# A decoder layer in split fp32: both MLP products by 2x2 blocks with seven block products, the squared activations kept in DRAM, the gate as a stage of its own

## The chip, the cores and the metric

The kernel runs on one core of one Trainium2 chip. The metric is device microseconds of one execution; the time before is the median of three runs. Engine names are those of the profile: PE is TensorE's matmuls, PEld its weight loads, DVE VectorE, ACT ScalarE, POOL GpSimd, SP the queue of SyncE that issues all DMAs.

## The reference

One layer of a hybrid decoder on 2048 tokens of 1024 channels. A token mixer (RWKV-7 beside a pooling mixer, both gated) gives `x1`; then come the squared-ReLU MLP, a gated embedding and a final norm. The change touches what follows the mixer:

```python
h = rmsnorm(x, g_mlp)                                   # 2048 x 1024
x = x + jnp.square(jax.nn.relu(h @ w_ff1)) @ w_ff2      # w_ff1 1024 x 4096, w_ff2 4096 x 1024
h = rmsnorm(x, g_ple)
x = x + jax.nn.sigmoid(h @ w_ple_gate) * (p @ w_ple_proj)   # p 2048 x 256
return rmsnorm(x, g_final)
```

## The kernel before

Every matmul operand is a pair of fp32r tiles, the rounded value ("hi", made by an ACT cast) and the rest ("lo", a subtraction on DVE or POOL). `mm3` multiplies a stationary pair by a moving pair in three matmuls: hi by hi, hi by lo, lo by hi. A moving operand is 512 columns wide, so all large matmuls are 128x128 by 128x512.

The order of PE is the order of the code (`manual_schedule`); a scheduler orders the other engines, each of which then works strictly in its order. PSUM has eight banks: four of tag `d` (`dps`), two of `rp` (`rps`), two of `rc` (`cps`).

The mixer fills the first half of the time. Its last part, `stage_B` of the fourth block of 512 tokens, projects with `yx` and `big` as operands (24 matmuls a group) and writes `x1` to DRAM (`x1D`). Between its groups, `head0` loads, normalises, transposes and splits the first eight tiles of 128 tokens into `hT2`.

Then the tokens go in two halves (`blk`) of 1024, eight tiles each. In a half, `w_ff1` is taken in 32 column tiles. `ff1` computes one tile for 1024 tokens (2 x 24 matmuls), squares on ACT and DVE and splits the result into `rt`. After four such tiles, `w_ff2`'s four row tiles are multiplied with them (192 matmuls) and added on DVE into `xa`, which holds the half's `x1` in SBUF. Weights come raw from DRAM and are split by `wsplit`: hi on ACT, lo half on DVE and half on POOL (L1099), into rings of two (`w1`) and four (`w2`) buffers.

In the last chunk of a half, `xa`'s tiles are normalised with `g_ple`, transposed between the matmuls and put back into `hT2`. The gate follows in the same half: `gate_mm` 24 matmuls and `put` 6 for each tile and each 512 columns, then tanh, product, sum, final norm and store. The weights of the gate are split in each half, in the rings of `w1`, `w2` and `rt`. The next half's norms and transposes lie between the gate's second eight groups.

Of the kernel before, what the change touches and what calls it, by code (L numbers as in the profile page):

```python
# [18 lines left out]
P = 128  # L19
T = 2048  # L20
# [78 lines left out]
def hybrid_kernel(ctx, tc, consts, x, p, g_mix, w_in, mu_shift, w0, w_decay_up, a0, w_aaa_up,  # L99
# [94 lines left out]


    with ExitStack() as c1:
        const = c1.enter_context(tc.tile_pool(name="const1", bufs=1, side="left"))
        fg = c1.enter_context(tc.tile_pool(name="fg", bufs=1, side="left"))

# [61 lines left out]
        c1r = ExitStack()  # L261
# [104 lines left out]
        big = fg.tile([P, 2, 8, TB], FR, name="big")  # L366
        yx = fg.tile([P, 2, 4, TB], FR, name="yx")
# [36 lines left out]
        def stage_A(b, nxt):  # L404
# [39 lines left out]
            def shifted(zi, m):  # L444
# [7 lines left out]
                ze = fg.tile([P, 15 + TB], F32, name="ze", tag="pl", bufs=3)  # L452
# [50 lines left out]
            for g, w in reversed(list(enumerate(WINS))):  # L503
# [3 lines left out]
                zp = fg.tile([P, W], F32, name="zp", tag="pl", bufs=3)  # L507
# [4 lines left out]
                while sh < w:  # L512
                    lo += sh
                    nx = fg.tile([P, W], F32, name="zs", tag="pl", bufs=3)
                    DVE.tensor_tensor(nx[:, lo:W], cur[:, lo:W], cur[:, lo - sh:W - sh], ALU.add)
                    cur, sh = nx, sh * 2
# [556 lines left out]
        gb = gvec(g_mlp[0])  # L1073

        def head0():
            xts = {}
            for j in range(NJ + 1):
                if j < NJ:
                    xts[j] = fg.tile([P, D], F32, name="xt", tag="wr", bufs=WR)
                    SP.dma_start(out=xts[j], in_=x1D[j * P:(j + 1) * P, :])  # L1080
                    norm_tile(fg, xts[j], gb, xts[j], dict(tag="t2k", bufs=5))
                    yield
                if j > 0:
                    transpose_split(xts.pop(j - 1), hT2, (j - 1) * P, cps)
                    yield

        w1p = ctx.enter_context(tc.tile_pool(name="w1p", bufs=1, side="right", reuse_waits="tile"))
        w1v = w_ff1[0].rearrange("(k p) c -> p k c", p=P)

        def wsplit(pool, src, k, n, wpool, tag, bufs):  # L1090
            raw = pool.tile([P, 1024], F32, name="wr", tag="wr", bufs=WR if pool is fg else 3)
            SP.dma_start(out=raw[:, 0:k * n].rearrange("p (k n) -> p k n", n=n), in_=src)
            wf = wpool.tile([P, 2, 1024], FR, name="wf", tag=tag, bufs=bufs)
            hi = wf[:, 0, 0:k * n]
            ACT.copy(out=hi, in_=raw[:, 0:k * n])  # L1095
            ws = WS3 if pool is not fg else k * n
            for eng, c in ((DVE, slice(0, ws)), (POOL, slice(ws, k * n))):
                if c.start < c.stop:
                    eng.tensor_tensor(wf[:, 1, c], raw[:, c], hi.bitcast(F32)[:, c], ALU.subtract)  # L1099
            return wf.rearrange("p s (k n) -> p s k n", n=n)  # L1100

        def w1tile(pool, m):
            return wsplit(pool, w1v[:, :, m * P:(m + 1) * P], 8, P, w1p, "w1", 2)

        hg = head0()
        for n, y in enumerate(stage_B(NB - 1, None)):
            if n >= 24 and n % 4 == 0:
                next(hg, None)
        for _ in hg:
            pass  # L1110
        w1pre = {m: w1tile(fg, m) for m in range(2)}
    f2 = ctx.enter_context(tc.tile_pool(name="f2", bufs=1, side="left", reuse_waits="tile"))
    if True:
        def wtile2(src, k, n, tag, bufs):
            return wsplit(f2, src, k, n, w1p if tag == "w1" else f2, tag, bufs)

        def tmp2():
            return f2.tile([P, 512], F32, name="t2", tag="t2", bufs=3)

        tjunk = dict(tag="t2", bufs=3)  # L1120
        w2v = w_ff2[0].rearrange("(k p) c -> p k c", p=P)
        wgv = w_ple_gate[0].rearrange("(k p) c -> p k c", p=P)
        wpv = w_ple_proj[0].rearrange("(k p) c -> p k c", p=P)
        xa = [None] * NJ

        def load_xa(blk, j):
            xa[j] = f2.tile([P, D], F32, name="xa", tag=f"xa{j}", bufs=1)
            SP.dma_start(out=xa[j], in_=x1D[blk * TC + j * P:blk * TC + (j + 1) * P, :])

        def norm_x(gbc, j, rows=None):  # L1130
            xn = f2.tile([P, D], F32, name="xn", tag="wr", bufs=3)
            src = xa[j]
            if rows is not None:
                src = xn
                SP.dma_start(out=xn, in_=x1D[rows, :])
# [11 lines left out]
        def ff1(ms, late=()):  # L1147
# [3 lines left out]
            for hf in range(TC // 512):  # L1151
# [207 lines left out]
```

## Time and profile before

| | |
|---|---|
| median of 3 runs | 3362.46 us (3361.72 to 3364.98) |
| profiled execution | 3362.13 us, span 3360.3 us, mean granted clock 0.98 |
| busy: PE, DVE, ACT, POOL | 3196.8 (95%), 2021.1 (60%), 1182.4 (35%), 950.1 us (28%) |
| moved by DMA | 485.60 MB, mean 145 GB/s |
| first half's MLP, gate | 1685 to 2361 us, 2361 to 2533 us of the span |
| second half's MLP, gate | 2533 to 3219 us, 3219 us to the end |

A row of a group reads: line, engine, operation, output<-inputs, shapes, count | busy us, mean ns of one | idle time of the engine just before them, and what ended it. Matmuls are pipelined, so the mean of one is longer than the distance of two. A row of the timeline begins with start and duration in us. In the slices a digit is the busy share in tenths.

### The profile page before, as it was taken

The numbers are of one execution on the slowest core, as the hardware profiler recorded it, in microseconds if no ns is written. First come the engines' busy times: TensorE is split into PE (matmuls) and PEld (weight loads), VectorE is DVE, ScalarE is ACT, GpSimd is POOL, SyncE is SP. The second block draws the span as 40 slices with busy tenths as digits, with TensorE's granted clock in tenths as the row PEclk, the third lists the DMA queues.
The fourth block names the chain that finished last, engine by engine and source line by source line (L and its number), as shares of the span: only waits on it lengthen the run. The fifth ranks groups of instructions, "written<-read, shape, count | busy, mean of one in ns | idle before, by whom it ended". The sixth has DMA issues, their size and how long they took to land.

```text
span 3360.3 us, 43232 instructions
## 1 busy us (share of the span) xinstructions
PE 3196.8 (95%) x15177; PEld 2620.5 (78%) x15177; DVE 2021.1 (60%) x5020; ACT 1182.4 (35%) x2406; POOL 950.1 (28%) x1162
## 2 busy tenths in 40 slices
PE   7989999999999997889899999999999999999998
PEld 6777777777878786668688888888788888888887
DVE  4489888788887879873643333333775333333375
ACT  4445544554455444431322222211332222221132
POOL 4655444344434435421111111111102111111110
PEclk9999999999999998999999999999999999999999
DMA  8866767666766567778741111110233111111021
GB/s 249 243 216 205 245 205 236 222 212 186 227 218 219 175 209 235 234 242 290 275 140 51 51 51 51 44 51 26 83 131 113 51 51 51 51 47 47 26 65 60
DMA packets 391030, 485.60 MB, mean 145 GB/s; under 512 B 168158, under 2 KB 298268, under 8 KB 367644
## 3 DMA queue, kind: packets, MB, share of 16 engines
q1 hardware_dynamic: 390812, 482.83, 45.1%
q8 instruction: 120, 1.97, 0.2%
q14 instruction: 98, 0.80, 0.1%
HBM read 363.21 MB, written 119.54 MB: 144 GB/s over the span
## 4 chain that ended last, share of the span: by engine, by line
PE 70%; DVE 14%; DMA 7%; ACT 3%; issue 3%; POOL 2%; SPq 1%; DVEq 0%; POOLq 0%; ACTq 0%
PE d L133 63%; DVE Xtmp L869 3%; PE rc L133 3%; PE rp L133 3%; DMA At<-aD 2%; DVE Xt L872 1%; ACT sq L961 1%; DMA aD<-Ast 1%; DMA wf<-wc 1%; DMA t2k<-yaD 1%; PE rp L137 1%; DVE wf L238 1%; DVE Apr L859 1%; PE rc L137 1%; SPq L789 0%
## 5 line engine op out<-in xcount | busy, mean ns | idle before, releaser
L133 PE MATMUL d<-big,wf 128*128 128x512 f32 (+1 forms) x3288 | 840.6, 403 | 17.6 <-DVE wf L238 9.2
L133 PEld LDWEIGHTS d<-big,wf 128*128 128x128 f32 x3288 | 608.9, 192 | 150.2 <-DVE wf L238 11.7
L133 PE MATMUL d<-wf,rt 128*128 128x512 f32 x3072 | 722.4, 395 | 0.0
L133 PE MATMUL d<-hT,wf 128*128 128x512 f32 x3072 | 700.1, 389 | 0.6 <-DVE hT L185 0.4
L133 PEld LDWEIGHTS d<-wf,rt 128*128 128x128 f32 x3072 | 574.9, 187 | 139.7
L133 PEld LDWEIGHTS d<-hT,wf 128*128 128x128 f32 x3072 | 576.5, 188 | 121.6 <-DVE hT L185 0.7
L1099 POOL TENSOR_TENSOR wf<-wr,wf 128x512 fp32r<-128x512 f32 x146 | 256.8, 1764 | 1396.1 <-ACT wf L1095 1394.5
L1215 DVE TENSOR_TENSOR xa<-xa,d 128x512 f32<-128x512 f32 x256 | 175.7, 686 | 410.0 <-PE d L133 409.6
L1095 ACT CAST wf<-wr 128x1024 fp32r<-128x1024 f32 x148 | 153.4, 1045 | 688.7 <-PE d L133 570.0
L1159 DVE TENSOR_TENSOR t<-t,d 128x512 f32<-128x512 f32 x128 | 87.9, 687 | 274.9 <-ACT t L1158 274.9
L869 DVE TENSOR_TENSOR Xtmp<-Xt,At 128x16 f32<-128x16 f32 (+15 forms) x512 | 238.3, 465 | 9.3
L133 PE MATMUL d<-yx,wf 128*128 128x512 f32 x768 | 210.0, 420 | 25.7 <-ACT yx L387 15.8
L133 PE MATMUL d<-wf,big 128*128 128x512 f32 x768 | 190.5, 401 | 11.0 <-DVE t2k L608 9.2
L1158 ACT ACTIVATE t<-d 128x512 f32<-128x512 f32 x128 | 76.6, 599 | 347.3 <-PE d L133 347.3
L133 PEld LDWEIGHTS d<-yx,wf 128*128 128x128 f32 x768 | 150.1, 202 | 62.1 <-ACT yx L387 17.5
L1099 DVE TENSOR_TENSOR wf<-wr,wf 128x512 fp32r<-128x512 f32 (+1 forms) x148 | 115.8, 783 | 131.3 <-ACT wf L1095 130.9
L133 PE MATMUL d<-wf,hT 128*128 128x512 f32 x768 | 183.6, 394 | 0.0
L1161 DVE TENSOR_TENSOR rt<-t,rt 128x512 fp32r<-128x512 f32 x128 | 154.0, 1203 | 45.3 <-ACT rt L1160 45.3
L133 PEld LDWEIGHTS d<-wf,big 128*128 128x128 f32 x768 | 143.0, 191 | 43.7 <-DVE t2k L608 11.1
L133 PEld LDWEIGHTS d<-wf,hT 128*128 128x128 f32 x768 | 143.9, 188 | 33.6
L872 DVE TENSOR_REDUCE Xt<-Xtmp 128x8 f32<-128x16 f32 (+15 forms) x512 | 147.5, 288 | 9.4
L238 POOL TENSOR_TENSOR wf<-wr,wf 128x640 fp32r<-128x640 f32 (+2 forms) x69 | 121.1, 1756 | 76.4 <-ACT wf L235 71.8
(225 smaller groups left out, 3921.3 us busy)
## 6 DMA issues: line engine op xcount, KB each, us to landing
wf<-wc SPq DMA_DIRECT2D x131, 1024.0 KB, 5.7
wr<-in_w_ff_dram SPq DMA_DIRECT2D x128, 512.0 KB, 4.0
wc<-wf SPq DMA_DIRECT2D x50, 1024.0 KB, 6.3
wr<-in_w_in_dram SPq DMA_DIRECT2D x51, 512.0 KB, 4.4
zD<-t2k SPq DMA_DIRECT2D x96, 256.0 KB, 4.7
zs<-zD SPq DMA_DIRECT2D x32, 640.0 KB, 6.4
At<-aD SPq DMA_DIRECT2D x32, 512.0 KB, 4.8
xt<-in_x_dram SPq DMA_DIRECT2D x28, 512.0 KB, 6.9
```

Source lines behind the costliest of these rows:

```text
L133: PE.matmul(out_, lhsT, rhs, start=start, stop=stop, **kw)
L137: PE.transpose(out_, in_, idn)
L238: eng.tensor_tensor(wf[:, 1, c], raw[:, c], hi.bitcast(F32)[:, c], ALU.subtract)
L859: DVE.tensor_tensor(pr, Ab[:, :, :, e:e + 1].broadcast_to([P, SUB, nb, lvl]), dgv[:, :, o:o + lvl].unsqueeze(1).broadcast_to([P, SUB, nb, ...
L869: DVE.tensor_tensor(tmp[:, :, :, 0:n], Xt[:, :, 0:n].unsqueeze(2).broadcast_to([P, MCOL, FS, n]), At[:, 0:n, r:n].rearrange("p s r -> p r ...
L872: DVE.tensor_reduce(Xt[:, :, r:n].unsqueeze(3), tmp[:, :, :, 0:n], AX.X, ALU.add)
L1095: ACT.copy(out=hi, in_=raw[:, 0:k * n])
L1099: eng.tensor_tensor(wf[:, 1, c], raw[:, c], hi.bitcast(F32)[:, c], ALU.subtract)
L1158: ACT.activation(out=t, in_=ps, func=AF.Relu)
L1159: DVE.tensor_tensor(t, t, ps, ALU.mult)
L1161: DVE.tensor_tensor(rt[:, 1, cs], t, rt[:, 0, cs].bitcast(F32), ALU.subtract)
L1215: DVE.tensor_tensor(xa[j][:, ns], xa[j][:, ns], ps, ALU.add)
```

## The change

Write the three matrices of a product as 2x2 blocks, with the tokens of a half split into two times 512 (indices `e`), and K and N split in two. Seven block products of sums replace the eight. For the left matrix A and the right B, with S1 = A21 + A22, S2 = S1 - A11, S3 = A11 - A21, S4 = A12 - S2:

P1 = A11 B11, P2 = A12 B21, P3 = S4 B22, P4 = A22 (B21 - t2), P5 = S1 (B12 - B11), P6 = S2 t2, P7 = S3 (B22 - B12), where t2 = B22 - B12 + B11. The result's blocks are P1 + P2; U2 + P5 + P3; U3 + P4; U3 + P5, with U2 = P1 + P6 and U3 = U2 + P7.

First product, 32 pairs (2 halves x 16): B's blocks alternate in column tiles of 128, so that a pair's two tiles stand side by side in memory (256 columns). The seven left operands of 512 columns stay split in SBUF ("home": four new tiles, `yx`, and both halves of `big`); each of a pair's seven products is 12 matmuls in one PSUM bank, in turn over all eight banks. `combine` loads the raw weights of a pair and makes the seven right operands one pair ahead, in a ring of 12 `op` tiles. `pair` adds the products up in seven temporaries (`t2`), cuts and squares them on DVE (L1256), makes the sums of the squared blocks on POOL (L1250 on POOL) and stores all seven to DRAM (`rD`, 256 KB each).

The second half's head (`heads1`) runs between the pairs 2 to 12 of the first half, two steps a pair, and stores its seven raw operands to DRAM (`hD`); after the last pair's product of each kind `load_home` loads and splits the operand of that product anew.

Second product, 56 steps (2 halves x 4 chunks of 8 row tiles x 7 products): a step is 48 matmuls into four banks. Its left operands come from `rD` (1 MB a step) and are split on ACT and POOL; the weights' sums are made in place on POOL, and split on ACT and DVE. A ring of 18 `op` tiles holds them, eight a step. DVE adds the four banks to accumulators in SBUF, in the last chunk also one product to another, and the result goes to DRAM (`x2D`).

The gate is a stage of its own over all 16 tiles of 128 tokens: the weights are split once, `norm_in` loads a tile of `x2D`, normalises, transposes and splits it three tiles ahead.

`yx`, `big` and the constants change their pools; up to the last output projection the order on every engine is as before.

The core of the diff (what is left out: the pools, the second half of `head` with its stores, loads that stand as described; of the removed code the functions above are shown already):

```diff
+        def combine(pool, pr, wrb, tmp):
+            raws = []
+            for h in range(2):
+                raw = pool.tile([P, 1024], F32, name="wr", tag="wr", bufs=wrb)
+                raw = raw.rearrange("p (k n) -> p k n", n=2 * P)
+                SP.dma_start(out=raw, in_=w1v[:, 4 * h:4 * h + 4, pr * 2 * P:(pr + 1) * 2 * P])
+                raws += [raw[:, :, 0:P], raw[:, :, P:2 * P]]
+            b11, b12, b21, b22 = raws
+            ops = {}
+            def op(nm, src, eng):
+                t = optile().rearrange("p s (k n) -> p s k n", n=P)
+                split((t[:, 0], t[:, 1]), src, eng)
+                ops[nm] = t
+            op("P1", b11, DVE)
+            op("P2", b21, POOL)
+            DVE.tensor_tensor(b11, b12, b11, ALU.subtract)
+            op("P5", b11, DVE)
+            t2 = tmp().rearrange("p (k n) -> p k n", n=P)
+            DVE.tensor_tensor(t2, b22, b11, ALU.subtract)
+            op("P6", t2, DVE)
+            POOL.tensor_tensor(b12, b22, b12, ALU.subtract)
+            op("P7", b12, POOL)
+            DVE.tensor_tensor(b21, b21, t2, ALU.subtract)
+            op("P4", b21, DVE)
+            if pool is fg:
+                return ops
+            op("P3", b22, POOL)
+            return ops
...
+        ops_next = combine(fg, 0, WR, t2k)
+        for nm in ("A22", "S4"):
+            for k in (slice(0, 2), slice(2, 4)):
+                split((home[nm][:, 0, k, :], home[nm][:, 1, k, :]), hraw[nm][:, k, :], DVE)
...
+    FIRST = dict(P1="A11", P2="A12", P3="S4", P4="A22", P5="S1", P6="S2", P7="S3")
+    def prod(ops, nm, last):
+        ps = pps()
+        h = home[FIRST[nm]]
+        for k in range(4):
+            mm3(ps, (ops[nm][:, 0, k, :], ops[nm][:, 1, k, :]), (h[:, 0, k, :], h[:, 1, k, :]), k == 0, k == 3)
+        if last:
+            load_home(FIRST[nm])
+        return ps
+    def pair(blk, pr, ops, last, between):
+        def relu2(t, nm):
+            DVE.scalar_tensor_tensor(t, t, 0.0, t, op0=ALU.max, op1=ALU.mult)
+            if nm:
+                put(nm, t)
+            return t
+        def put(nm, t):
+            SP.dma_start(out=rD[blk][nm][:, pr, :], in_=t)
+        ps = prod(ops, "P1", last)
+        p1 = tmp2()
+        ACT.copy(out=p1, in_=ps)
+        u2 = add(tmp2(), p1, prod(ops, "P6", last))
+        r11 = relu2(add(p1, p1, prod(ops, "P2", last)), "A11")
+        u3 = add(tmp2(), u2, prod(ops, "P7", last))
+        between()
+        ps = prod(ops, "P5", last)
+        r22 = relu2(add(tmp2(), u3, ps), "A22")
+        add(u2, u2, ps)
+        r21 = relu2(add(u3, u3, prod(ops, "P4", last)), None)
+        s1 = add(tmp2(), r21, r22, POOL)
+        put("S1", s1)
+        s3 = add(r21, r11, r21, POOL, ALU.subtract)
+        put("S3", s3)
+        s2 = add(tmp2(), s1, r11, POOL, ALU.subtract)
+        put("S2", s2)
+        r12 = relu2(add(u2, u2, prod(ops, "P3", last)), "A12")
+        put("S4", add(tmp2(), r12, s2, POOL, ALU.subtract))
...
+    def operands(blk, c, nm, w):
+        raw = hr()
+        SP.dma_start(out=raw, in_=rD[blk][FIRST[nm]][:, c * KC:(c + 1) * KC, :])
+        res = []
+        for p_ in range(KC):
+            a = optile()
+            split((a[:, 0, :], a[:, 1, :]), raw[:, p_, :], POOL)
+            e, o = w[p_, 0], w[p_, 1]
+            b11, b12, b21, b22 = e[:, lo], e[:, hi], o[:, lo], o[:, hi]
+            if nm == "P5":
+                POOL.tensor_tensor(b11, b12, b11, ALU.subtract)
+            elif nm == "P6":
+                POOL.tensor_tensor(b11, b22, b11, ALU.subtract)
+            elif nm == "P7":
+                POOL.tensor_tensor(b12, b22, b12, ALU.subtract)
+            elif nm == "P4":
+                POOL.tensor_tensor(b21, b21, b11, ALU.subtract)
+            b = optile()
+            split((b[:, 0, :], b[:, 1, :]), dict(P1=b11, P2=b21, P5=b11, P6=b11, P7=b12, P4=b21, P3=b22)[nm], DVE)
+            res.append((a, b))
+        return res
...
+    seq = [(blk, c, nm) for blk in range(NBLK) for c in range(NCH) for nm in ORDER]
+    nxt = operands(0, 0, "P1", w2[0])
+    for n, (blk, c, nm) in enumerate(seq):
+        cur = nxt
...
+        pss = [dps() for _ in range(4)] if n % 2 == 0 else [rps(), rps(), cps(), cps()]
+        for p_, (a, b) in enumerate(cur):
+            for j in range(4):
+                ts = slice(j * P, (j + 1) * P)
+                mm3(pss[j], (a[:, 0, ts], a[:, 1, ts]), (b[:, 0, :], b[:, 1, :]), p_ == 0, p_ == KC - 1)
+        for j in range(4):
+            acc = accs[nm][j]
+            if c == 0 and nm in ("P1", "P5", "P6", "P7"):
+                ACT.copy(out=acc, in_=pss[j])
+            else:
+                DVE.tensor_tensor(acc, acc, pss[j], ALU.add)
...
+    def norm_in(j):
+        xt = f4.tile([P, D], F32, name="xt", tag="xt", bufs=2)
+        SP.dma_start(out=xt, in_=x2D[j * P:(j + 1) * P, :])
+        norm_tile(f4, xt, gb, xt, dict(tag="t4", bufs=4))
+        hts[j] = ht = f4.tile([P, 2, 8, P], FR, name="ht", tag="ht", bufs=4)
+        for h in range(2):
+            pt = cps()
+            for k in range(4):
+                tr(pt[:, k * P:(k + 1) * P], xt[:, (4 * h + k) * P:(4 * h + k + 1) * P], ident)
+            ks = slice(4 * h, 4 * h + 4)
+            split((ht[:, 0, ks, :], ht[:, 1, ks, :]), pt.rearrange("p (k t) -> p k t", t=P), DVE)
...
+    gb = gvec(g_ple[0])
+    norm_in(0)
+    for q in range(4):
+        weights(wgv, wgs, g4, q, "wg")
+    norm_in(1)
+    weights(wpv, wps, f4, 0, "wp")
+    gfin = f4.tile([P, D], F32, name="gfin")
+    SP.dma_start(out=gfin, in_=g_final.unsqueeze(0).broadcast_to([P, D]))
+    for j in range(2):
+        load_x2(j)
+    embed(0)
+    norm_in(2)
+    wait = []
+    for j in range(NT):
+        if j + 3 < NT:
+            norm_in(j + 3)
+        if j + 1 < NT:
+            embed(j + 1)
+        if j + 2 < NT:
+            load_x2(j + 2)
+        for n in range(2):
+            wait.append((j, n, gate(j, n)))
+            while len(wait) > (1 if j + 1 < NT else 0):
+                put(*wait.pop(0))
```

Three places in the order. DVE in the first product. Before, in the second half (`t` the square's temporary, `rt` its split, `wf` and `wr` weights, `xa` the sum):

```order
L1159 TENSOR_TENSOR t_18488<-t_18488,d 128x512
L1161 TENSOR_TENSOR rt<-t_18488,rt 128x512
L1159 TENSOR_TENSOR t_18518<-t_18518,d 128x512
L1099 TENSOR_TENSOR wf<-wr,wf 128x512
L1161 TENSOR_TENSOR rt<-t_18518,rt 128x512
L1215 TENSOR_TENSOR xa<-xa,d 128x512 x15
```

Now, a pair of the second half from its third product on (`t` the temporaries, read beside a PSUM bank d, rp or rc; `op` weights' splits; `wr` raw weights):

```order
L1250 TENSOR_TENSOR t_21438<-t_21407,d 128x512
L1181 TENSOR_TENSOR t_21467<-wr 128x512
L1185 TENSOR_TENSOR wr<-wr,t_21467 128x4x128
L1103 TENSOR_TENSOR op<-t_21467,op 128x512
L1250 TENSOR_TENSOR t_21496<-t_21438,d 128x512
L1250 TENSOR_TENSOR t_21407<-t_21407,d 128x512
L1256 SCALAR_TENSOR_TENSOR t_21496<-t_21496 128x512
L1250 TENSOR_TENSOR t_21438<-t_21438,rp 128x512
L1178 TENSOR_TENSOR wr<-wr 128x4x128
L1256 SCALAR_TENSOR_TENSOR t_21438<-t_21438 128x512
L1250 TENSOR_TENSOR t_21407<-t_21407,rp 128x512
L1256 SCALAR_TENSOR_TENSOR t_21407<-t_21407 128x512
```

A pair's sums of products now stand in one line with the next pairs' weights; R21 (`t_21438`) is cut behind the weights' sums, R12 (`t_21407`) last. (Three splits of `op` between these rows are left out, since they read alike.)

POOL at the same place. Before, its last mixer work and then only halves of weights' splits:

```order
L609 TENSOR_TENSOR t2k<-t2k 128x512 x3
L946 TENSOR_TENSOR sq_16094<-Y 128x256
L609 TENSOR_TENSOR t2k<-t2k 128x512
L963 TENSOR_TENSOR sq_16211<-sq_16211,bon 128x256
L964 TENSOR_TENSOR sq_16211<-sq_16211,gg 128x256
L609 TENSOR_TENSOR t2k<-t2k 128x512 x8
L1099 TENSOR_TENSOR wf<-wr,wf 128x512 x146
```

Now, the end of that pair and of the one behind it:

```order
L1103 TENSOR_TENSOR op<-wr,op 128x512 x2
L1183 TENSOR_TENSOR wr<-wr 128x4x128
L1250 TENSOR_TENSOR t_21516<-t_21438,t_21496 128x512
L1250 TENSOR_TENSOR t_21438<-t_21405,t_21438 128x512
L1250 TENSOR_TENSOR t_21521<-t_21516,t_21405 128x512
L1250 TENSOR_TENSOR t_21540<-t_21407,t_21521 128x512
```

Two splits and a sum of weights stand ahead of S1 (`t_21516`), then S3, S2 and S4 in a row.

PE where the gate begins. Before, in the first half (`xn` and `pt` are transposed):

```order
L133 MATMUL d<-wf,rt 128x512 x6
L137 MATMUL rp<-ident,pt 128x128 x2
L133 MATMUL d<-wf,hT_16370 128x512 x42
L137 MATMUL rc<-ident,xn 128x128 x8
L133 MATMUL d<-wf,hT_16370 128x512 x6
```

Now:

```order
L133 MATMUL rp<-op 128x512 x6
L133 MATMUL rc<-op 128x512 x6
L137 MATMUL rc<-ident,xt 128x128 x16
L137 MATMUL rc<-ident,pt 128x128 x2
L133 MATMUL d<-wg_27490,ht 128x512 x3
```

The gate's first matmul stood among the last transposes; now four tiles' transposes (the rows of 16 and 2 come twice) stand between the second product's last matmul and it, all through the two banks of `rc`.

More of the change, by code (lines that the diff above doesn't have):

```diff
@@ L1073, in hybrid_kernel @@
         gb = gvec(g_mlp[0])
[L1075 to L1085, printed above, removed]
@@ L1106, in hybrid_kernel, with heads0, load @@
+        def heads0():
+            def load():
+                return [fg.tile([P, D], F32, name="xt", tag="wr", bufs=WR) for _ in range(2)]
+            for j in range(4):
+                yield from head(0, j, fg, load, t2k, dict(tag="t2k", bufs=5), (rps, cps))
+        hraw = {nm: hr() for nm in ("A22", "S4")}
+        hg = heads0()
         for n, y in enumerate(stage_B(NB - 1, None)):
-            if n >= 24 and n % 4 == 0:
+            if n >= 34 and n % 3 == 0:
                 next(hg, None)
@@ new lines, in hybrid_kernel, with load_home @@
+    SP.dma_start(out=raw, in_=w1v[:, 4:8, P:2 * P])
+    t = optile().rearrange("p s (k n) -> p s k n", n=P)
+    split((t[:, 0], t[:, 1]), raw, POOL)
+    ops_next["P3"] = t
+    def load_home(nm):
+        raw = hr()
+        SP.dma_start(out=raw, in_=hD[nm])
+        for k, eng in ((slice(0, 2), DVE), (slice(2, 4), POOL)):
+            split((home[nm][:, 0, k, :], home[nm][:, 1, k, :]), raw[:, k, :], eng)
+    FIRST = dict(P1="A11", P2="A12", P3="S4", P4="A22", P5="S1", P6="S2", P7="S3")
+    banks = [0]
@@ new lines, in heads1, with load, between @@
+    def heads1():
+        def load():
+            t = hr((P, 2, D))
+            return [t[:, 0, :], t[:, 1, :]]
+        for j in range(4):
+            yield from head(1, j, f2, load, tmp2, dict(tag="t2", bufs=NT2), (dps, dps))
+    hg = heads1()
+    pairs = [(blk, pr) for blk in range(NBLK) for pr in range(NPR)]
+    for n, (blk, pr) in enumerate(pairs):
+        ops = ops_next
+        def between():
+            later.append(combine(f2, pairs[n + 1][1], 3, tmp2) if n + 1 < len(pairs) else None)
+        later = []
+        pair(blk, pr, ops, blk + 1 < NBLK and pr == NPR - 1, between)
+        ops_next = later[0]
+        if blk == 0 and pr >= 2:
+            next(hg, None)
+            next(hg, None)
@@ new lines, in hybrid_kernel, with weights @@
+    c3.close()
+    g4 = ctx.enter_context(tc.tile_pool(name="g4", bufs=1, side="right", reuse_waits="tile"))
+    f4 = ctx.enter_context(tc.tile_pool(name="f4", bufs=1, side="left", reuse_waits="tile"))
+    wgv = w_ple_gate[0].rearrange("(k p) c -> p k c", p=P)
+    wpv = w_ple_proj[0].rearrange("(k p) c -> p k c", p=P)
+    wgs, wps, hts, pts, xs, fss = {}, {}, {}, {}, {}, {}
+    NT = T // P
+    def weights(view, res, pool, q, nm):
+        raw = hr()
+        SP.dma_start(out=raw.rearrange("p (k n) c -> p k (n c)", n=2), in_=view[:, 2 * q:2 * q + 2, :])
+        for i in range(4):
+            k, n = divmod(i, 2)
+            t = pool.tile([P, 2, 512], FR, name=f"{nm}{2 * q + k}{n}")
+            split((t[:, 0, :], t[:, 1, :]), raw[:, i, :], (DVE, POOL)[n])
+            res[2 * q + k, n] = t
@@ new lines, in embed, with load_x2 @@
+    def embed(j):
+        pt = f4.tile([P, 256], F32, name="pt", tag="pt", bufs=2)
+        SP.dma_start(out=pt, in_=pv[j * P:(j + 1) * P, :])
+        ps = cps()
+        for k in range(2):
+            tr(ps[:, k * P:(k + 1) * P], pt[:, k * P:(k + 1) * P], ident)
+        pts[j] = f4.tile([P, 2, 256], FR, name="pT", tag="pT", bufs=3)
+        split((pts[j][:, 0, :], pts[j][:, 1, :]), ps[:, 0:256], DVE)
+    def load_x2(j):
+        xs[j] = f4.tile([P, D], F32, name="x2", tag="x2", bufs=4)
+        SP.dma_start(out=xs[j], in_=x2D[j * P:(j + 1) * P, :])
```

404 lines of the change are left out of this document (187 added, 217 removed).

## The prediction

> **What bounds the kernel now.** I read the engine totals and the slices first, then the table by stretches for the part that is changed, then the chain of waits there, then the groups, and last single rows of the timeline. All durations come from the profiled execution: 3362.13 us by its own clock, span 3360.3, beside a median of 3362.46; the sum below is made against 3362.1.
>
> ```profile
> PE 3196.8 (95%) x15177; PEld 2620.5 (78%) x15177; DVE 2021.1 (60%) x5020; ACT 1182.4 (35%) x2406; POOL 950.1 (28%) x1162
> ...
> PE   7989999999999997889899999999999999999998
> ```
>
> ```profile
> 1685.00:2361.00 676.00, 676.00 (x2942) 551.35 (x2941) 245.65 (x325) 138.32 (x199) 110.30 (x62) 1.00 0.19 57
> 2361.00:2533.00 172.00, 170.68 (x807) 138.56 (x805) 131.97 (x433) 67.95 (x136) 19.29 (x12) 1.00 0.38 123
> 2533.00:3219.00 686.00, 685.50 (x2991) 558.95 (x2992) 262.35 (x382) 146.03 (x216) 115.10 (x65) 1.00 0.17 50
> 3219.00:3361.00 142.00, 131.29 (x594) 105.97 (x592) 82.43 (x244) 38.55 (x79) 12.07 (x7) 0.98 0.19 66
> ```
>
> The four stretches are the MLP and the gate of each half of the tokens; the columns after the length are PE, PEld, DVE, ACT, POOL, granted clock, DMA share and GB/s. From 1685 on PE is busy without a hole at full clock, while DVE is busy 36% of the time, POOL 16%, and DMA runs at 50 to 60 GB/s. The chain of waits says the same: two runs of matmuls that wait for nothing.
>
> ```profile
> 1676.42 684.98 PE d L133 x2979
> ...
> 2533.32 665.25 PE d L133 x2891
> ```
>
> ```profile
> L133 PE MATMUL d<-wf,rt 128*128 128x512 f32 x3072 | 722.4, 395 | 0.0
> L133 PE MATMUL d<-hT,wf 128*128 128x512 f32 x3072 | 700.1, 389 | 0.6 <-DVE hT L185 0.4 <-ACT hT L184 0.3
> ...
> L133 PE MATMUL d<-wf,hT 128*128 128x512 f32 x768 | 183.6, 394 | 0.0
> ```
>
> 684.98/2979 and 665.25/2891 both give 0.230 us a matmul (the 390 ns of a single one overlap). So a matmul less in this part is 0.230 us less, as long as PE stays fed. That is the whole question: the change takes matmuls from PE and gives work to DVE, POOL and DMA, of which there was little.
>
> **The matmuls.** 6144 matmuls of the two products become 32 pairs x 7 x 12 = 2688 and 56 steps x 48 = 2688. The 768 that go are 768 x 0.230 = -176.6 us. The gate's 768 + 192 and all 256 transposes of normalised rows stay (64 in the head, 64 for the second half, 128 in the gate stage). All that stands before the last output projection stands in the same order, so the first 1600 us stay.
>
> **DVE, POOL and what they share.** A pair takes PE 84 x 0.230 = 19.3 us. In that time DVE has 18 operations of 128x512 (7 that read a product in PSUM, 11 that read two SBUF tiles), POOL 8 of two SBUF tiles, ACT 8 casts or copies, and 9 DMAs go out. Their prices:
>
> ```profile
> L1099 POOL TENSOR_TENSOR wf<-wr,wf 128x512 fp32r<-128x512 f32 x62 | 110.3, 1785 | 580.6 <-ACT wf L1095 580.6
> ...
> L1161 DVE TENSOR_TENSOR rt<-t,rt 128x512 fp32r<-128x512 f32 x64 | 77.0, 1203 | 23.3 <-ACT rt L1160 23.3
> L1215 DVE TENSOR_TENSOR xa<-xa,d 128x512 f32<-128x512 f32 x112 | 76.9, 687 | 201.5 <-PE d L133 201.5
> L1099 DVE TENSOR_TENSOR wf<-wr,wf 128x512 fp32r<-128x512 f32 x62 | 44.8, 723 | 58.7 <-ACT wf L1095 58.5
> ...
> L1160 ACT CAST rt<-t 128x512 fp32r<-128x512 f32 x64 | 39.7, 620 | 26.4 <-DVE t L1159 26.4
> ```
>
> The 1785 and the 1203 ns are not prices. The timeline, and a larger operation with nothing beside it, show what they are:
>
> ```profile
> 1803.00 0.69 DVE L1161 TENSOR_TENSOR rt<-t,rt 128x512 fp32r<-128x512 f32 x1 [0.69 <-ACT rt L1160]
> ...
> 1808.00 0.69 DVE L1099 TENSOR_TENSOR wf<-wr,wf 128x512 fp32r<-128x512 f32 x1 [0.25 <-ACT wf L1095]
> 1808.05 1.80 POOL L1099 TENSOR_TENSOR wf<-wr,wf 128x512 fp32r<-128x512 f32 x1 [9.08 <-ACT wf L1095]
> 1808.61 1.79 DVE L1161 TENSOR_TENSOR rt<-t,rt 128x512 fp32r<-128x512 f32 x1
> ```
>
> ```profile
> 3240.65 1.28 DVE L1222 SCALAR_TENSOR_TENSOR xn<-xa,rs_yn,gb 128x1024 f32<-128x1024 f32 x1
> 3240.84 2.25 POOL L1099 TENSOR_TENSOR wf<-wr,wf 128x512 fp32r<-128x512 f32 x1 [23.62 <-ACT wf L1095]
> 3241.86 1.78 DVE L1099 TENSOR_TENSOR wf<-wr,wf 128x512 fp32r<-128x512 f32 x1
> ```
>
> ```profile
> L218 POOL TENSOR_TENSOR xt<-xt,gmix 128x1024 f32<-128x1024 f32 x2 | 4.7, 2344 | 2.2 <-ACT junk L160 2.2
> ```
>
> POOL's 1.80 us are 0.64 of waiting until DVE's first operation ends at 1808.69, and 1.16 of work; DVE's second ends 0.55 after POOL's end. Once more at 3240: 1.09 of waiting and 1.16 of work. Half of 2344 ns is 1.17. DVE operations on PSUM keep 687 ns whatever POOL does. So an operation of DVE on two SBUF tiles and one of POOL exclude each other; I take 1.18 for POOL and 0.65 for DVE (0.69 alone, 0.61 from start to start in a row). The Trainium skill, "SBUF — State Buffer", section "SBUF: two separate sides", speaks against this change: the two engines share one port pair under "an **exclusive lock**", held for the whole instruction, while the other is blocked. By that rule the sum is the one below; were both to run side by side, each at its row's mean, it would be that of the second rival.
>
> Shared time per pair: 11 x 0.65 + 8 x 1.18 = 16.6 of 19.3 us. In the second product a chunk of 7 steps has 28 splits and 16 sums of weights on POOL and 28 splits on DVE: 44 x 1.18 + 28 x 0.65 = 70.1 of 77.3 us. Both fit, the second with 9% to spare; steps with sums need 8 x 1.18 + 4 x 0.65 = 12.0 of 11.0, but operands are made almost two steps ahead, so four such steps (4 us) are carried by the three light ones. I cost the second product at +6 us, bounds 0 and 60 (were POOL to idle 10% in its order).
>
> **The loop of a pair.** DVE works in order, and its first operation of a pair (the sum of the first two products) writes into the buffer of the pair before that holds S1; it waits until POOL has made S1 and its store has landed, and until S2 is made. From that operation to the sign-cut of R21 lie 15 operations of DVE, 9.8 us; four POOL operations fall between them and block about 4; casts on ACT add some 0.7; then S1 takes 1.2. That is 15.7 us and the store. Stores of this size:
>
> ```profile
> mbD<-t2k SPq DMA_DIRECT2D x32, 256.0 KB, 2.0
> ...
> x1D<-t2k SPq DMA_DIRECT2D x32, 256.0 KB, 4.3
> ```
>
> ```profile
> 400.00:1200.00 800.00, 751.27 (x3981) 622.36 (x3982) 670.30 (x1997) 411.85 (x980) 331.67 (x544) 0.97 0.67 211
> ...
> 1500.00:1600.00 100.00, 96.89 (x466) 80.29 (x464) 42.31 (x92) 21.06 (x50) 17.13 (x16) 1.00 0.84 286
> ```
>
> The loop is 17.7 to 20.0 us; S1, S3 and S2 in a row on POOL give 18.2 as the least. I take 3 us for the store, since a pair moves 2.75 MB in 19.3 us, an estimate of 142 GB/s, below the 211 to 286 of the stages where these rows were measured: 18.7, under PE's 19.3. Steady pairs cost +3, bounds 0 and 22 (32 x 0.7).
>
> The second half's head lies in ten of these pairs: 8 normalisations and 12 sums on DVE, 4 on POOL.
>
> ```profile
> L155 DVE SCALAR_TENSOR_TENSOR rs_yn<-rs_qn,rs_yn 128x1 f32<-128x1 f32 x156 | 27.3, 178 | 2.7
> ...
> L1222 DVE SCALAR_TENSOR_TENSOR xn<-xa,rs_yn,gb 128x1024 f32<-128x1024 f32 x16 | 20.5, 1283 | 0.9
> ```
>
> 8 x (1.28 + 13 x 0.1, the small ones lying half inside each other's waits) + 12 x 0.65 + 4 x 1.18 = 33 us, 3.3 a pair: the loop becomes 22.0, 2.7 too long, 27 in ten pairs. PE can run ahead about 8 us, until it needs the next pair's P6 operand: 19 are left. At the turn of the halves seven operands are loaded and split again (7 x (1.23 + 2.34) us of the shared time, twice the prices above); most of it has slack: +8. Together +27, bounds 10 and 45.
>
> **The turns.** (a) Into the first product. The last projection ran without a hole into it:
>
> ```profile
> 1634.61 5.24 PE L133 MATMUL d<-wf,big 128*128 128x512 f32 x21
> ...
> 1676.17 9.12 PE L133 MATMUL d<-wf,big 128*128 128x512 f32 x39
> ```
>
> In these 51 us lie now 8 norms (some 3.2 us with their waits, 26), 24 sums and splits of 0.65 (16), 16 residual sums (10), four splits of twice the size (5) and 7 operations for the first pair (5) on DVE, beside POOL's 15 of 1.18, which block a few: some 66 us. Part of it can begin before, and the projection ends about 10 later; P6's operand stands behind four splits of `big`, which wait for the last projection: PE waits 5 more. +15, bounds 5 and 30. (b) Into the second product: three of four operand pairs fit in free buffers early: +3, bounds 0 and 10. (c) Into the gate. The third and fourth tiles' transposed operands lie where the last sums (P3) stood, whose store must land first: 4 us of sums, 3 of store, then two rounds of transpose, cast, split through two PSUM buffers, 5.5: +13.5, bounds 8 and 25. The gate itself has 60 matmuls a tile, 13.8 us, against about 11 of DVE, and no POOL. (d) What stalled there before goes: 1.3 us in the second stretch, and in the fourth 10.7 less the 9.3 behind the last matmul, which stay: -2.7.
>
> ```profile
> 3349.42 1.55 PE L133 MATMUL rp<-wf,rt 128*128 128x512 f32 x6
> ```
>
> (e) Holes cost clock:
>
> ```profile
> 1600.00:1607.00 7.00, 0.16 (x1) 0.00 (x0) 0.01 (x1) 0.62 (x1) 0.00 (x0) 0.54 0.94 334
> 1607.00:1612.00 5.00, 4.99 (x13) 3.70 (x14) 1.58 (x3) 0.63 (x1) 1.27 (x1) 0.62 0.40 136
> ```
>
> After a hole of 7 us the next 5 run at a clock of 0.62: about 2 us lost. Two such holes: +4, bounds 2 and 6.
>
> At nothing I cost ACT (8 x 0.62 = 5 us a pair) and the extra traffic (3 MB a pair at most, 11 MB a chunk, an estimate of 142 GB/s in each), which lies beside PE; SP issues 9 DMAs a pair. If that cover goes, the S1 store is late first.
>
> **Sum.** -176.6 + 15 + 3 + 27 + 3 + 6 + 13.5 - 2.7 + 4 = -107.8: 3362.1 - 107.8 = 3254. All lower ends give 3208, all upper ends 3381.
>
> **Rivals.** *DVE's loop sets the pair.* If the S1 store takes 4.3 or more, or POOL's two splits ahead of S1 come late, a pair takes some 20.7 and the head's pairs 24: +45 instead of 3 and +40 instead of 27, 3254 + 55 = 3309. For it speaks that 0.6 us is all that separates the two; against it the idle DMA. *POOL is as slow as its row says.* If 1785 ns is POOL's own price, six to seven of its operations in the loop add 3.9 us a pair (22.6; 32 x 3.3 = 106), and a chunk needs 44 x 1.785 + 18.2 = 96.7 (8 x 19.4 = 155): 3254 - 9 + 261 = 3506, slower. It decides from a price of 1.5, where 208 x 0.32 - 19 and 8 x (66 + 18.2 - 77.3) eat up the gain. Against it stand the 2344 ns of twice the size and both timeline rows. *It is hidden.* PE's lead takes up head and turns but for the gate's: 3215. That the change doesn't do what it says is no case: the order has 2688 and 2688 matmuls.
>
> **Chances.** The sum 0.65 (own range 3225 to 3290); the loop 0.14; hidden 0.10; POOL's price, or anything else that ends slower, 0.11. Of the first three a little lands near zero. Range: 3212 to 3335, from the hidden case past the loop's. Faster by over 0.2% (about what a measurement of this kernel can tell from no change) 0.86, within it 0.02, slower 0.12. Predicted: 3254 us.
>
> **What would show it.** In the changed profile: runs of 84 matmuls in 19.3 us in the late pairs, and PE waiting for DVE in pairs 3 to 15 alone; POOL rows of 128x512 near 1.2 us where DVE stands still and near 1.8 where it doesn't; 48 matmuls in 11.0 us through the chunks; holes of 10 to 15 us at the first product and ahead of the gate. Wrong would be the loop if PE waits in every pair with u2 waiting for the S1 store; the price of POOL if P5, P6, P7 steps grow past 12 us; and the sum as a whole if the order makes one engine wait for another in a way that I did not follow.

## The result and the profile after

The changed kernel takes 3463.55 us (median of 4, 3458.82 to 3463.86) beside 3363.72 us of the kernel before in the same series: ratio 1.0294, 95% interval 1.0276 to 1.0312. It is slower by 2.9%, where 3.2% faster was forecast. The profiled execution has a span of 3461.9 us, 101.6 more than before; its time is 209 us above the sum of the prediction. One execution of the last kernel below took 3837 us, at a granted clock of 0.74, and is in none of the figures.

The totals and the first line of the slices of the changed kernel:

```profile
PE 3093.9 (89%) x14409; PEld 2515.9 (73%) x14409; DVE 2473.3 (71%) x5424; ACT 1336.5 (39%) x2774; POOL 1669.3 (48%) x1657
...
PE   7999999999999988798788898999899999957678
```

PE has its 768 matmuls less, but it is busy only 103 us less instead of 177, and its idle time grew by 204 us (163.5 to 368.0): it stands still, and where it works it is in part slower. The slices show where: the sevens and eights in the middle, and the last five. The table by stretches has the last output projection, the first half's pairs with the first pair of the second, the other pairs, the second product, the way into the gate, and the gate (columns as before):

```profile
1641.00:1721.00 80.00, 59.62 (x250) 46.22 (x248) 54.83 (x148) 33.33 (x57) 23.15 (x15) 0.87 0.45 154
1721.00:2135.00 414.00, 354.50 (x1493) 284.19 (x1494) 312.42 (x450) 113.04 (x190) 232.82 (x149) 0.92 0.53 176
2135.00:2426.00 291.00, 291.00 (x1260) 236.51 (x1260) 195.72 (x262) 66.56 (x117) 165.60 (x117) 1.00 0.44 150
2426.00:3055.00 629.00, 616.66 (x2689) 504.67 (x2687) 469.76 (x476) 267.10 (x481) 546.03 (x358) 0.99 0.48 170
3055.00:3092.00 37.00, 9.01 (x37) 6.82 (x36) 28.99 (x81) 15.89 (x29) 8.98 (x6) 0.55 0.70 266
3092.00:3461.00 369.00, 268.36 (x1086) 212.58 (x1085) 159.76 (x513) 70.91 (x159) 0.00 (x0) 0.86 0.18 61
```

Two stretches came as forecast. In the late pairs PE is busy without a hole at full clock, 15 pairs in 291 us, 19.4 each (19.3 forecast). In the second product two rows of the chain of waits show steps of 48 matmuls in 10.9 us, and 56 steps take 629 us, 11 more than 2688 x 0.230 (9 forecast):

```profile
2548.55 10.88 PE d L133 x48
...
2570.36 10.92 PE d L133 x48
```

Most of the loss lies in three places where rows are normalised: the way into the first product, the first half's pairs and the gate. Who PE waits for, in the first half's pairs and in the gate (total us, times, longest):

```profile
PE d L137 <- DVE hr L173: 39.1, 6, 9.8
```

```profile
PE rc L137 <- DVE xt L173: 85.6, 12, 7.2
```

L137 are the transposes, L173 the norm's last operation on DVE. The chain of waits through one tile of the gate ("issue" is time in which the engine waited for nothing that the profile shows):

```profile
3201.03 0.49 ACT t L1474
3201.52 5.90 issue
3207.42 0.12 ACT junk L1481
3207.55 0.41 issue
3207.96 0.19 ACT junk L1481
3208.14 1.05 ACT junk L160 x2
3209.19 0.02 issue
3209.22 0.17 DVE nmsn L165
...
3211.53 1.30 DVE xt L173
3212.82 0.14 issue
3212.96 1.10 PE rc L137 x4
```

Read it from below: the transposes wait for the scaled rows, these for the root (twelve more small operations, left out here), the root for the square that sums up the row (L160, output `junk`), and that stands on ACT behind the square of the final norm of the tile before (L1481). Its rows were there long before: their load went out at 3190.4 us, 17.6 before the square, and in the first run below a square starts 3.5 us after its load went out. So the norm "three tiles ahead" begins only when the tile before is done, and then nothing lies beside it. A tile takes 25.3 us instead of 13.8 and its transposes.

Why L160 has this place in ACT's order is not in the trace. Its unused output takes a buffer of `t4`, the ring of four that tanh and the final square use; in the head it takes one of `t2` (seven temporaries of the pair) or `t2k` (five temporaries of the mixer). The first theory, R, is that this ring sets the order. The rival, L: the norm's small operations are late of themselves, in DVE's queue.

### The profile page after: what moved, and what is told of

The parts are those of the page before. It is cut to its first block, busy times and chain, and to the rows that moved or that the text cites. A ratio compares the mean times of both kernels' runs of the same rounds, so it can differ in the third digit from the quotient of the medians.

```text
span 3461.9 us, 44299 instructions
## 1 busy us (share of the span) xinstructions
PE 3093.9 (89%) x14409; PEld 2515.9 (73%) x14409; DVE 2473.3 (71%) x5424; ACT 1336.5 (39%) x2774; POOL 1669.3 (48%) x1657
## 5 line engine op out<-in xcount | busy, mean ns | idle before, releaser
L1103 DVE TENSOR_TENSOR op<-w,op 128x512 fp32r<-128x512 f32 x224 | 300.6, 1361 | 129.6 <-ACT op L1102 127.6
L1103 POOL TENSOR_TENSOR op<-hr,op 128x512 fp32r<-128x512 f32 x224 | 340.3, 1537 | 68.0 <-ACT op L1102 67.9
L133 PE MATMUL d<-op 128*128 128x512 f32 x1344 | 313.9, 392 | 8.9 <-ACT op L1102 5.1
L133 PEld LDWEIGHTS d<-op 128*128 128x128 f32 x1344 | 253.0, 189 | 65.3 <-ACT op L1102 5.5
L1103 POOL TENSOR_TENSOR op<-wr,op 128x512 fp32r<-128x512 f32 x96 | 139.3, 1460 | 212.5 <-ACT op L1102 212.5
L133 PE MATMUL d<-yx,wf 128*128 128x512 f32 x768 | 208.5, 418 | 21.2 <-ACT yx L390 13.8
L133 PE MATMUL d<-wg,ht 128*128 128x512 f32 x768 | 199.1, 417 | 0.0
L1250 POOL TENSOR_TENSOR t<-t,t 128x512 f32<-128x512 f32 x128 | 188.8, 1485 | 10.9 <-issue 5.6
L133 PEld LDWEIGHTS d<-wg,ht 128*128 128x128 f32 x768 | 153.9, 203 | 36.8
L133 PE MATMUL rp<-op 128*128 128x512 f32 x672 | 172.4, 391 | 2.8 <-POOL op L1103 2.8
L133 PE MATMUL rc<-op 128*128 128x512 f32 x672 | 171.1, 390 | 0.6 <-DVE accP L1384 0.6
```

What stands on the lines that cost most here:

```text
L133: PE.matmul(out_, lhsT, rhs, start=start, stop=stop, **kw)
L1103: eng.tensor_tensor(dst[1], src, dst[0].bitcast(F32), ALU.subtract)
L1250: eng.tensor_tensor(out_, a, b, op)
```

## The experiments

All runs start from the changed kernel. A run without an interval is one execution; the kernel before took 3352.5 to 3363.6 us beside these (nine executions).

**A ring of its own for the gate's square.**

```diff
-        norm_tile(f4, xt, gb, xt, dict(tag="t4", bufs=4))
+        norm_tile(f4, xt, gb, xt, dict(tag="jn", bufs=2))
```

> In the gate stage the square that sums up a row for its norm writes its unused output to a ring of two buffers of its own, instead of the ring of four temporaries (t4) that tanh and the final square use. Theory R (the ring): ACT can start that square only when the ring has come round, so it stands behind the final square of the tile before, and PE waits 7.1 us a tile; with a ring of its own the twelve holes of 7.1 us fall below 2 us, a tile takes 14 to 16 us instead of 25.3, the stage from the last matmul of the second product to the end 270 to 300 us instead of 407, the total 3330 to 3355. Theory L (latency and load): the chain behind the square (thirteen small DVE operations, scaling, transpose, cast, split) is itself as long as the hole, and DVE is late with it; the ring changes only the 1.7 us in front, total 3430 to 3465.

3371.8 us. The same place in the timeline:

```profile
3201.61 1.06 ACT L160 ACTIVATE junk<-xt 128x1024 bf16<-128x1024 f32 x1 [1.50 <-DMA xt<-x2D]
...
3208.00 0.63 ACT L1481 ACTIVATE junk<-x 128x512 bf16<-128x512 f32 x1 [5.24 <-DVE x L1477]
...
3213.94 0.30 PE L137 MATMUL rc<-ident,xt 128*128 128x128 f32 x1 [0.48 <-DVE xt L173]
```

The square now stands ahead of the final one and waits for its own load alone; PE's wait falls from 7.1 to 0.5 us, a tile from 25.3 to 16.9, and from the first gate matmul to the last it is 260.5 us instead of 359.1. No operation was removed: 98.6 us hung on which ring an output that nobody reads is put in. R is shown for the gate. The time stays 17 us above the expected range; two holes of 0.5 and 1.0 us are left in a tile:

```profile
PE rc L137 <- DVE ht L1103: 11.9, 12, 1.3
PE rc L137 <- DVE xt L173: 5.6, 11, 0.8
```

The table shows the second cost of the holes, the clock: 0.86 in the gate before this edit, 0.98 after it. PE is busy 244 us with the same work instead of 268.

```profile
3099.00:3369.00 270.00, 244.14 (x1085) 193.22 (x1084) 138.71 (x507) 67.64 (x157) 0.00 (x0) 0.98 0.23 83
```

The Trainium skill, "TensorE: Matmul & The Clock Gate", section "Part 1: The HAM clock gate", says that the array falls back to half its clock after an idle window of about 3.4 us. The trace agrees as far as it goes: in the 4 us behind the hole that ends at 3213.0 us the granted clock is 0.50, and with holes of 1 us the mean stays at 0.98.

**The entry into the gate.** On top of that, three buffers for the rows, one for the square's output, and two tiles ahead instead of three:

```diff
-        xt = f4.tile([P, D], F32, name="xt", tag="xt", bufs=2)
+        xt = f4.tile([P, D], F32, name="xt", tag="xt", bufs=3)
...
-        norm_tile(f4, xt, gb, xt, dict(tag="t4", bufs=4))
+        norm_tile(f4, xt, gb, xt, dict(tag="jn", bufs=1))
...
-    norm_in(2)
...
-        if j + 3 < NT:
-            norm_in(j + 3)
+        if j + 2 < NT:
+            norm_in(j + 2)
```

> On top of g1_gate_ring: three buffers for the loaded rows instead of two (and one for the norm's unused output), and the gate runs two tiles ahead instead of three. Theory of the gate's entry: the 37 us from the second product's last matmul to the gate's first are two rounds of load, norm and transpose, because only two tiles of rows can be loaded and four must be transposed ahead of the first gate matmul; with one round the gap falls to 20 to 26 us and the total by 11 to 17 us against g1_gate_ring (3372), to 3355 to 3361. Rival: the gap is the weights' load and split, which stay; gap 33 to 38 us, total 3368 to 3374. A tile's 16.9 us should stay either way.

3352.6 us; the gap between second product and gate falls from 37.3 us to 29.4, between the ranges of the theory (20 to 26) and its rival (33 to 38). So 8 us hung on the second round of load and norm, less than expected. The total is no evidence here: it fell by 19 us, but 15 of them are an earlier start of the first product, which this edit doesn't reach. A tile stays at 16.9 us, two tiles ahead or three.

**The head in the pairs: the ring alone.** The norm's square writes into the tile that takes the raw operands later:

```diff
+                if blk:
+                    ACT.activation(out=grp[:, 2 * e:2 * e + 2, :].rearrange("p a b -> p (a b)"), in_=x_, func=AF.Square, accum_out=ss)
...
```

> Between the pairs of the first product the norm's square writes its unused output into the tile that later holds the head's raw operands, not into the ring of the seven temporaries t2. Theory R: the squares wait for a t2 buffer (they start 20 us after their rows have landed), the holes before the head's transposes (39 us in all) fall below 15 us, total 3425 to 3440. Theory L: the norm's small operations stand in DVE's full queue, behind the pair's sums and POOL's operations; holes stay at 30 to 45 us, total 3450 to 3470.

3455.4 us: 8 less, inside L's range. The holes before the head's transposes fall from 39.1 to 29.5 us, just under L's 30 to 45 and far from R's 15. The first of four steps of the head lost its hole of 9.8 us (pair 3, counted from 0: 32.4 to 23.5 us); in the second and the fourth they stayed, 11 and 16 us. These have too little lead by the order itself: a step of the head is five pieces, two pieces go behind each pair, so that there the second norm and the first transposes lie behind the same pair. What such a norm meets on DVE is seen in the timeline of the changed kernel:

```profile
1981.23 0.15 DVE L153 TENSOR_TENSOR rs_qn<-rs_yn 128x1 f32<-128x1 f32 x1
1981.42 1.15 DVE L154 TENSOR_TENSOR rs_qn<-rs_qn,rs_hn 128x1 f32<-128x1 f32 x1
1982.61 1.18 DVE L155 SCALAR_TENSOR_TENSOR rs_yn<-rs_qn,rs_yn 128x1 f32<-128x1 f32 x1
1983.83 2.25 DVE L173 SCALAR_TENSOR_TENSOR hr<-hr,rs_yn,gb 128x1024 f32<-128x1024 f32 x1
```

```profile
1981.29 1.26 POOL L1183 TENSOR_TENSOR wr<-wr 128x512 f32<-128x512 f32 x1 [2.52 <-DVE rs_yn L155]
1982.52 1.26 POOL L1250 TENSOR_TENSOR t<-t,t 128x512 f32<-128x512 f32 x1
1983.73 1.26 POOL L1103 TENSOR_TENSOR op<-wr,op 128x512 fp32r<-128x512 f32 x1
```

An operation on 128x1 takes 0.15 us, and 1.15 when a POOL operation runs: it ends when POOL's ends. Between the norm's thirteen small operations stand fourteen larger ones, of the pair's sums, the weights and the head's own sums, 10 us in all. From L165 at 1970.9 to L173's end at 1986.1 the chain took 15 us; in the gate, without POOL and without these, it takes 3.6.

**Lead for the head.** The pieces spread over pairs 0 to 14, two pairs between norm and transpose (one in the last step); the second run with the ring of the run above:

```diff
+    LEAD = {0: 2, 2: 1, 3: 1, 4: 3, 6: 1, 7: 1, 8: 3, 10: 1, 11: 1, 12: 3, 13: 1, 14: 2}
...
-        if blk == 0 and pr >= 2:
-            next(hg, None)
-            next(hg, None)
+        if blk == 0:
+            for _ in range(LEAD.get(pr, 0)):
+                next(hg)
```

> The second half's head is spread over pairs 0 to 14 so that both norms of a step stand two pairs (the last: one) ahead of their transposes on PE, instead of one pair or none; the squares still write to the t2 ring. Theory L (norms of thirteen small operations take some 15 us in DVE's queue between the pair's sums, and PE meets its transposes before that): holes before the head's transposes fall from 39 to under 8 us, the sixteen pairs of the first half from 413 to 365 us or less, total 3410 to 3425. Theory R (the squares wait for a t2 buffer, whatever the lead): holes stay above 25 us, total above 3440.

> As h2_head_lead, and the squares write into the tile of the head's raw operands (as in h1_head_ring). If lead alone is what lacks, the same as h2_head_lead within 5 us; if the ring matters too, 10 us or more below it.

3453.5 and 3454.1 us. Where there are two pairs of lead the holes are gone: the first 13 pairs take 272 and 276 us instead of 314. The last step, with one pair, now has the hole (16 and 14 us), and the pair at the turn of the halves grew from 41 to 49 and 45. The first 17 pairs fall from 413 to 401 and 398 us, so that the totals miss L's 3410 to 3425; they stay where R had put them, but not for R's reason, since the holes follow the lead. The ring adds 3 us to it: here L holds, R little.

**Two pairs of lead for all four steps**, which end in pair 12, with the ring:

```diff
+    LEAD = {0: 2, 2: 1, 3: 4, 5: 1, 6: 4, 8: 1, 9: 4, 11: 1, 12: 2}
```

> As h3_head_lead_ring, but all four steps of the second half's head, the last too, have two pairs between norm and transpose, and the head ends in pair 12. If lead is what the last step lacked (14 us of hole in h3_head_lead_ring), no hole before a head's transposes is over 4 us and the first half's pairs fall from 407 (sum of the first 17 in h3) to 385 to 392, total 3432 to 3442. If the head's work on DVE and POOL is what costs, and the hole only shows where, the sum stays within 5 us of 407.

3429.4 us; the first 17 pairs take 384.7, as the lead theory said (385 to 392), and the hole of the last step is gone. The total is 34 less than the changed kernel's, of which 5 are an earlier start of the first product.

**What the second half's head costs in all.** Head and reload are left out; the second half multiplies the first half's operands.

> The second half's head and the reload of the left operands are left out: the second half multiplies the first half's operands once more (part of the computation is missing). This prices them as a whole. By the prediction's terms (27 us, and 64 transposes of 0.11 us) 3463 falls to 3425 to 3435. By the trace of the changed kernel (holes of 39 us before the transposes, some 17 us more at the turn of the halves, the transposes, and slow clock behind each hole) the first sixteen pairs fall from 413 to about 315 us, total 3360 to 3385.

3388.5 us; the first product falls from 704.4 to 625.8 us, and the first 16 pairs from 372 to 315. So the part that the prediction priced at 27 us, and PE's 7 us of transposes, cost 79.

**The start of the first product.** The first half's head writes its squares into the operand ring, which is empty then:

```diff
+                if blk:
+                    norm_tile(pool, x_, gb, x_, junk)
+                else:
...
+                    jn = hx.tile([P, 1024], F32, name="jn", tag="op", bufs=6)
+                    ACT.activation(out=jn, in_=x_, func=AF.Square, accum_out=ss)
...
```

> Between the groups of the last output projection the first half's head writes the unused output of its squares to the still empty operand ring, not to the five t2k temporaries that the residual's loads and sums use as well. Theory R: the holes of PE from 1641 to 1722 us (24 us in all) fall below 10 us and the first product starts 15 to 25 us earlier, total 3438 to 3450. Theory L: DVE's chain of norms and splits is what PE waits for; the first product starts within 8 us of where it did, total 3455 to 3470.

3448.6 us. The stretch of the projection, which took 80 us with 59.6 of PE:

```profile
1641.00:1704.00 63.00, 53.31 (x247) 42.94 (x247) 38.99 (x90) 27.89 (x48) 22.41 (x15) 0.92 0.56 191
```

The first product starts at 1704.9 instead of 1721.8 (1712.8 to 1727.9 in the nine runs that leave this ring as it was). Much of that scatter is older than the head: from the 300th last matmul of the projections, at 1602.2 in the changed kernel, to the first product it takes 119.6 us there, 115.6 to 122.3 in the nine runs, and 104.0 to 104.8 in this run and the two below that contain this edit. So the ring is worth 11 to 18 us, and R holds here. The squares took buffers that the residual's loads were waiting for: the queue's longest waits ahead of these loads (L635, for a `t2k` buffer in DVE's use) fall from 21.0 us in two waits to 10.4.

**POOL and DVE.** One POOL operation more in every step of the second product:

```diff
+        sc = f3.tile([P, 512], F32, name="sc", tag="sc", bufs=2)
+        POOL.tensor_tensor(sc, raw[:, 0, :], raw[:, 1, :], ALU.subtract)
```

> Each of the second product's 56 steps gets one more POOL operation on two SBUF tiles of 128x512, whose result nobody reads. If POOL and DVE exclude each other on SBUF, a chunk of seven steps has 51 x 1.2 to 1.26 + 28 x 0.67 = 80 to 83 us of the shared time against 77.3 of matmuls, and the second product grows from 629 us by 20 to 45 us, total 3483 to 3510. If POOL works beside DVE, it has 51 x 1.26 = 64 of 77 us to do, the second product stays within 8 us, total 3455 to 3471. If POOL's price were the 1.5 us of its rows' mean, 51 x 1.5 = 76.5 would just fit as well.

3506.7 us; the second product takes 673.5 us instead of 629.2, 84.2 a chunk. POOL is busy through nearly all of it:

```profile
2422.00:3096.00 674.00, 634.52 (x2692) 511.81 (x2690) 483.41 (x473) 257.25 (x481) 631.03 (x414) 0.97 0.45 159
```

51 x p + 28 x 0.67 = 84.2 gives p = 1.28 us, POOL's 1.26 in the timeline: times of both engines add up. Side by side 51 x 1.26 = 64 would have lain hidden. Nor is POOL slow by itself: in this stretch 102 of its operations meet none of DVE's on two SBUF tiles and take 1.29 us (median), the 297 others 1.74. So the Trainium skill's rule of the exclusive lock ("SBUF — State Buffer", section "SBUF: two separate sides") agrees with this run. This only bears on the second product's margin: by 44 x 1.26 + 28 x 0.67 = 74 of 77.3 us it was just wide enough.

The same in the first product: four of a pair's eight POOL operations go to DVE.

```diff
-            op("P2", b21, POOL)
+            op("P2", b21, DVE)
...
-            POOL.tensor_tensor(b12, b22, b12, ALU.subtract)
-            op("P7", b12, POOL)
+            DVE.tensor_tensor(b12, b22, b12, ALU.subtract)
+            op("P7", b12, DVE)
...
-            op("P3", b22, POOL)
+            op("P3", b22, DVE)
```

> In the first product the four POOL operations on weights of a pair (three splits, one sum) go to DVE; the rest as in the changed kernel. If POOL and DVE exclude each other, DVE now has 15 x 0.67 and POOL 4 x 1.27 = 15.1 us of the shared time a pair instead of 11 x 0.67 + 8 x 1.27 = 17.5, although DVE is busy 2.7 us longer: steady pairs stay at 19.4, the first 17 pairs fall from 413 by 15 to 40 us, total 3420 to 3448. If DVE's own busy time is what the head's pairs wait for, they grow by 2 us each, total 3470 to 3485.

3455.2 us, but the first 17 pairs take 413.5 us as before: neither theory. Most of the 8 us came from an earlier start of the first product (1714.4, within the scatter of the other runs). While the norms had no lead, less shared time did nothing.

**All together**, and the reload's splits on DVE alone:

```diff
-        for k, eng in ((slice(0, 2), DVE), (slice(2, 4), POOL)):
+        for k, eng in ((slice(0, 2), DVE), (slice(2, 4), DVE)):
```

> g3_gate_lead, s1_start_ring and h4_head_even together, and the reload of the left operands at the turn of the halves split on DVE alone. By the single runs: 110 us from the gate, 15 from the start, 20 to 30 from the head, 5 from the turn: 3463 falls to 3300 to 3315, faster than the kernel before by 1.4 to 1.9%. If the gains are not independent (a stage that comes earlier meets another wait), 3320 to 3345.

> c1_all_orders with the move of d1_combine_dve. If POOL and DVE exclude each other, 5 to 20 us below c1_all_orders; if DVE's busy time is the limit, 10 us or more above it.

| | median, us | ratio to before | first 17 pairs | gate, first to last matmul |
|---|---|---|---|---|
| changed kernel | 3463.55 | 1.0294 (1.0276 to 1.0312) | 413.1 | 359.1 |
| all orders | 3298.43 | 0.9823 (0.9807 to 0.9840) | 373.5 | 262.1 |
| and four POOL operations to DVE | 3278.85 | 0.9773 (0.9755 to 0.9791) | 352.5 | 261.4 |

All orders end 2 us below the range expected, the last kernel 20 us below that (5 to 20 expected). The pair at the turn of the halves, 42.7 us with the even lead, takes 32.5 with all orders and the reload's splits on DVE. With the lead in place the move that did nothing by itself is worth 21 us in the pairs. Both beat the kernel before, by 1.8% and 2.3%; the last one's stretches are the first half's pairs, the others, the second product, the entry and the gate:

```profile
1701.00:2053.00 352.00, 343.49 (x1490) 276.67 (x1491) 329.20 (x511) 108.37 (x183) 111.36 (x69) 0.99 0.60 197
2053.00:2345.00 292.00, 292.00 (x1264) 237.20 (x1264) 243.89 (x332) 69.91 (x123) 94.11 (x63) 1.00 0.47 159
2345.00:2975.00 630.00, 616.67 (x2689) 505.45 (x2687) 469.26 (x476) 268.05 (x481) 541.37 (x358) 0.99 0.48 170
2975.00:3005.00 30.00, 7.19 (x31) 5.37 (x29) 23.90 (x68) 12.62 (x24) 5.70 (x4) 0.56 0.85 328
3005.00:3277.00 272.00, 243.93 (x1094) 192.99 (x1092) 145.56 (x526) 71.07 (x165) 3.08 (x2) 0.99 0.23 82
```

## Why the prediction was wrong, point by point

- **The matmuls, -176.6, held**: 2688 and 2688, 0.227 to 0.231 us each where PE was fed (10.9 us for 48, 291 for 15 pairs).
- **POOL, DVE and the steady pairs held.** POOL's price is 1.26 us, not 1.18, and not the 1.785 of the rival; the pairs took 19.4, and the loop of the S1 store never showed. Into the second product and through it, +9 forecast, +11 measured.
- **The gate, term (c), is the step that failed.** Counted from the start of the two products (1685.1), gate, transposes and tail before take 1675.2 - 6144 x 0.230 = 262 us; less 7 of the second half's transposes and with the forecast's +10.8 this makes 266, and from the second product's last matmul to the end it was 406.7: 141 of the 209 us. The step that was wrong is that PE sets the tile, at 13.8 us; a tile took 25.3. "13.8 us, against about 11 of DVE" compared busy times. DVE was indeed idle more than half of the stage. What set the tile was the chain from the final square of one tile to the norm of the next, and the order of ACT that the ring brought about. That PE has the transposes directly behind `put` stands in the loop that the prediction worked from; it does not ask which work of ACT stands ahead of them.
- **The second half's head, +27, took 71** (386.6 us for pairs 1 to 16, less 16 x 19.3 and 7 of transposes). As a price of the work the sum was near: by the same count it is 32 us with all orders, and 14 with fewer POOL operations. What was missed is the lead: none or one pair, against a chain that takes 15 us in DVE's queue.
- **The start, +15, took 44** (36.7 later, and 7 in the first pair). 11 to 18 us of it are the ring of `t2k`. Another 9 were lost earlier, where the prediction has the first 1600 us stay: the 300th last matmul of the projections starts at 1602.2 instead of 1593.3. PE waits 6.5 us for DVE there, between 1550 and 1561, instead of 1.7; why is open.
- **The clock, term (e), +4 for two holes**, was too small for a hole in every tile of the gate: PE's busy time there is 24 us longer than in the first run, for the same work. It lies inside the 141.
- **The rivals**: none was it. (The terms of the hidden one give 3254 - 27 - 15 - 3 = 3209, not 3215, which changes nothing.) "Slower" came true, but not by POOL's price; a slower tile of the gate was in no case, and the range (3212 to 3335) left no room for one. What the prediction named last as a sign of being wrong, one engine waiting for another by the order, is what happened.

What stays open: why the scheduler put L160 behind L1481, though the buffer that it waits for should be free earlier by a count of the ring. That the ring decides it is shown, and that one buffer of its own is enough; the rule by which is not, nor whether a larger common ring would do as well. Nor was the entry's remaining 29 us taken apart.

## What to carry to other kernels

When work is moved to a place of its own, nothing lies beside it any more: follow one round of its chain through all engines, in the order that each will have, before comparing busy times. An output that nobody reads still occupies a buffer; put it in a ring of its own, or it can tie work that should run ahead to the work that it runs ahead of (98.6 us in the gate here, a few between the pairs). And give a chain of small operations that passes through a full queue a lead counted in its length there (15 us), not in its length alone (3.6 us).

## What the runs showed of the hardware

- A DVE operation of 128x1 with two inputs in SBUF takes 0.15 us, and took 1.15 to 1.18 where a POOL operation of 1.26 us ran: it ended with POOL's, small as it is.
- POOL's subtraction of 128x512 takes 1.26 us where DVE's takes 0.67: a pair with 15 + 4 of them (DVE's and POOL's on two SBUF tiles) instead of 11 + 8 needs 2.4 us less of the time that the two share by this sum, an estimate, though DVE is busier. In the pairs it was worth 21 us in 17 pairs, once the norms had lead, and nothing before.
- Holes of 7.1 us every 25 us brought the mean granted clock to 0.86, and to 0.50 in the 4 us behind one of them; with holes of about 1 us or less every 17 us it was 0.98.
